# Four kinds of norm weights: broadcast loads replaced by one-row loads and products with ones

## The chip, the cores and the metric

The kernel runs on one core of one Trainium2 chip. The metric is the device time of one execution in microseconds; the time of a kernel is the median of its runs. One execution is also recorded by the hardware profiler. Its trace counts time from the start of its span, and all moments below ("at 655 us") are moments of that trace.

## The reference, cut to what matters

One layer of a streaming encoder runs over 2048 prompt rows and 128 sample rows (17 tiles of 128 rows, tile 16 being the sample rows). Half of the mixer is an HGRN2 gated recurrence, the other half is chunk-band attention. Then come an output projection, a squared-ReLU MLP and a final norm. Everything is float32. The change concerns the weights `g` of three of the norms.

```python
def rmsnorm(x, g):
    xf = x.astype(jnp.float32)
    y = xf * lax.rsqrt(jnp.mean(xf * xf, axis=-1, keepdims=True) + EPS)
    return (y * g.astype(jnp.float32)).astype(x.dtype)
...
    o_a = rmsnorm(o_a.reshape(B, T, ATT_WIDTH), att_norm_g)
    x = x + jnp.concatenate([o_h, o_a.astype(x.dtype)], axis=-1) @ w_out
    u = rmsnorm(x, norm2_g) @ w_up
    x = x + jnp.square(jax.nn.relu(u)) @ w_down
...
    y_prompt = rmsnorm(xp, final_norm_g)
    y_sample = rmsnorm(xs, final_norm_g)
```

`att_norm_g` has 512 elements, `norm2_g` and `final_norm_g` have 1024 each. Rows lie on the 128 partitions, so each weight must stand on all partitions to be multiplied in.

## The kernel before, in words

The work runs in three phases, one after the other in the program: `phase_hgrn`, `phase_att`, `phase_mlp`. Inside a phase, generators are woven together by written costs (`weave`), and the framework orders each engine's instructions from that program; every engine then runs its own list strictly in that order. Memory of a phase's pools goes to the next phase's pools, so a first write to a new tile may have to wait for the last use of an old one.

- Every large product is done in a split precision: `mm3` (L365 to L374) issues three TensorE products for each pair of a high and a low part, L370, L371 and L372. A weight block is loaded by L300 or L334 into `wraw` (2 buffers of 1024 columns), then split by ScalarE into `whi` (L321) and by VectorE into `wlo` (L322), in 8 buffers of 512 columns each.
- The recurrence, `hgrn_tile` (L545 to L667), handles one tile of 128 rows: levels of small products (L573, L580) alternate with VectorE steps on `sc`, `qp` and `ks` (L581, L594, L595), then come the output (L616, L618), the state (L621, L626), a norm (ScalarE L658, GpSimd L90 and L92) and the scaled output `ob` (L663). `c.state` is stored by L630 after the last tile.
- `phase_att` (L1052 to L1086) projects q, k and v of groups of three tiles (`att_proj_group`, from L974), runs the attention (`att_group`, from L772) and the output projection (`out_group`, L931, `out_tile`, L948), woven together. The first product of its program is the q projection of the first group. Its PSUM pool `c.ps_mm` has 3 buffers. `att_finish` (L764) multiplies each finished tile by `c.again`, the spread `att_norm_g` (L768).
- `prepare` (L1096) norms tiles of the residual with `norm2_g` (ScalarE L100, GpSimd L90 and L92, VectorE L125) and transposes them into `h_hi` and `h_lo` for the MLP (`transpose_split`, L108: TensorE L115, ScalarE L117, VectorE L118, in two halves of four transposes). For the first six tiles it runs beside the last output projection of `phase_att`, with the weight in a late tile, `g2` (L1100, L1102).
- `phase_mlp` (L1145) loads `norm2_g` once more (`c.g2`, L1159) and `final_norm_g` (`gf`, L1160), used by later `prepare` calls and by `finish` (L1164). `sample_mixer` (L1114) does the attention of the sample rows beside the first MLP group and loads `att_norm_g` again (L1119).

Before, `gain_tile` (L64) and L1102 load each weight with a DMA that reads the same row for each of the 128 partitions: 256 KB for `att_norm_g`, 512 KB for the others. There are five such loads, all on SP's queue. A second helper, `gain_rows` (L71), is used once, for the norm weights of the recurrence (`hgain`, L714): it loads one row to partition 0, then a product of a row of 128 ones with that row writes it to all partitions in PSUM (L80, `grow_ps`, 512 columns at a time), and ScalarE copies it back over the tile (L81).

Of the kernel before, what the change touches and what calls it, by code (L numbers as in the profile page):

```python
# [8 lines left out]
F32 = mybir.dt.float32  # L9
# [8 lines left out]
P = 128  # L18
D = 1024
# [33 lines left out]
def consts(c, pool):  # L53
# [5 lines left out]
    c.r1 = pool.tile([P, NTT], F32, name="r1")  # L59
    c.mhalf = pool.tile([P, 8], F32, name="mhalf")  # L60
    nc.gpsimd.memset(c.mhalf, -0.5)


def gain_tile(c, pool, name, a):  # L64
    n = a.shape[-1]
    t = pool.tile([P, n], F32, name=name)
    c.nc.sync.dma_start(out=t, in_=a.broadcast_to([P, n]))
    return t


def gain_rows(c, t, a, ps_pool, tag):  # L71
# [980 lines left out]
def phase_att(c):  # L1052
    tc, nc = c.tc, c.nc
    GMAX = max(len(x) for x in GROUPS) * P
    with ExitStack() as s:
        def pool(name, bufs, **k):
            return s.enter_context(tc.tile_pool(reuse_waits="tile", name=name, bufs=bufs, **k))
        cp = pool("a_const", 1)
        c.qsp = pool("a_qs", 4)
        c.qp_ = pool("a_q", 5)  # L1060
        c.vp = pool("a_v", NV - 3)
        c.krp = pool("a_kr", 2)
        c.ob = pool("a_ob", 2)
        c.pt = pool("a_pt", 2)
        c.sp = pool("a_s", 2)
        c.yo = pool("a_yo", 3)
        c.ps_mm = pool("a_psmm", 3, space=PSUM)
        c.ps_po = pool("a_pspo", 1, space=PSUM)
        c.ps_tx, c.ps_tx_tag = c.ps_mm, "mm"
        c.ps_s = pool("a_pss", 2, space=PSUM)  # L1070
        kw = 2 * (512 + GMAX)
        flat = c.h0p.tile([P, HN], F32R, tag="h_hi", name="K012")
        c.K = [flat[:, i * kw:(i + 1) * kw] for i in range(3)] + [cp.tile([P, kw], F32R, tag="K3", name="K3")]
        c.K = [x.rearrange("p (e n) -> p e n", e=2) for x in c.K]
        c.again = gain_tile(c, cp, "again", c.att_g)
        c.late = lambda: cp.tile([P, kw], F32, tag="K3", name="g2")[:, :D]
        gs = [Ctx() for _ in GROUPS]
        for g in gs:
            g.nk, g.nv, g.done, g.q, g.fin = 0, False, 0, [None] * 4, False

        def att():
            yield LAG
            for g, tiles in zip(gs, GROUPS):
                yield from att_group(c, g, tiles)

        run(weave(att_proj(c, gs), 19.5, att(), 13.5))  # L1086
# [9 lines left out]
def prepare(c, tiles, g, ready=None, g2=None):  # L1096
    if ready:
        while not ready():
            yield None
        g2 = g2()  # L1100
        h_tiles(c.h0p, g)
        c.nc.sync.dma_start(out=g2, in_=c.norm2_g.broadcast_to([P, D]))  # L1102
    else:
        g2 = c.g2
    for j, t in enumerate(tiles):
        x2 = c.xin.tile([P, D], F32, tag="x", name="x2")
        c.nc.sync.dma_start(out=x2, in_=c.x1[t * P:(t + 1) * P, :])
        norm_rows(c, x2, g2, x2)
        both = c.ps_s.tile([P, 2, 512], F32, tag="S", name="tx2") if ready else None
        transpose_split(c, x2, g.hi, g.lo, j * P, both=both)  # L1110
        yield 1.0


def sample_mixer(c):  # L1114

    tc, nc = c.tc, c.nc
    with ExitStack() as s:
        c.smp = s.enter_context(tc.tile_pool(reuse_waits="tile", name="s_smp", bufs=1))
        c.again = gain_tile(c, c.smp, "again", c.att_g)  # L1119
        qbd = c.smp.tile([P, 4, 8, 32], F32, name="qbd")  # L1120
        qs = c.smp.tile([P, 4, P], F32, name="qs")
        ksam = c.smp.tile([P, 4, P], F32, name="ksam")
        vsam = c.smp.tile([P, 512], F32, name="vsam")
        nc.gpsimd.memset(qbd, 0.0)
        nc.sync.dma_start(out=qs, in_=c.sq.rearrange("f p t -> p f t"))
        nc.sync.dma_start(out=ksam, in_=c.sk.rearrange("f p t -> p f t"))
        nc.sync.dma_start(out=vsam, in_=c.sv)
        for e in range(2):
            src = slice(64 * e, 64 * e + 64)
            nc.gpsimd.tensor_copy(qbd[src, :, :, 16 * e:16 * e + 16],  # L1130
                                  qs[src].rearrange("p f (b t) -> p f b t", b=8))
        yield from att_sample(c, qbd, ksam, vsam)
    with ExitStack() as s:
        op = s.enter_context(tc.tile_pool(reuse_waits="tile", name="s_oT", bufs=1))
        c.yo = s.enter_context(tc.tile_pool(name="s_yo", bufs=3))
        wp = s.enter_context(tc.tile_pool(name="s_w", bufs=4))
        o = OT(c, [14, 15, NPT])
        o.hi, o.lo = (op.tile([P, KT, 3 * P], F32R, name="sT_" + x) for x in ("hi", "lo"))
        o.pre(2)
        yield 1.0  # L1140
        for w in out_group(c, o, None, wp):
            yield 0.12 * w


def phase_mlp(c):  # L1145
# [3 lines left out]
    with ExitStack() as s:  # L1149
        def pool(name, bufs, **k):  # L1150
            return s.enter_context(tc.tile_pool(reuse_waits="tile", name=name, bufs=bufs, **k))
        cp = pool("m_const", 1)
        yp = pool("m_y", 7)
        up = pool("m_u", 1)
        wp = pool("m_u2", 2)
        c.ps_mm = pool("m_psmm", 4, space=PSUM)
        c.ps_tx, c.ps_tx_tag = pool("m_pstx", 2, space=PSUM), "tx"
        c.ps_smp = pool("m_pssmp", 2, space=PSUM)
        c.g2 = gain_tile(c, cp, "g2", c.norm2_g)  # L1159
        gf = gain_tile(c, cp, "gf", c.final_g)  # L1160

        pend = []

        def finish(t, y):  # L1164
            norm_rows(c, y, gf, y, "y")
            nc.sync.dma_start(out=rows(c, c.y_p, c.y_s, t), in_=y)

        def mlp(tiles, g):
            n = len(tiles) * P
            ys = []  # L1170
            for fc in range(DFF // FC):
                wu = next(c.ws)
                uh = up.tile([P, FC // P, GMAX], F32R, tag="uh", name="uh")
                ul = up.tile([P, FC // P, GMAX], F32R, tag="ul", name="ul")
                for f, cs, ps in proj_fm(c, wu, g, n, 1):
                    cn = cs.stop - cs.start
                    u2 = wp.tile([P, 384], F32, tag="u2", name="u2")[:, :cn]
                    nc.scalar.activation(u2, ps, AF.Relu)  # L1178
                    nc.vector.scalar_tensor_tensor(out=u2, in0=ps, scalar=0.0, in1=u2,  # L1179
                                                   op0=ALU.max, op1=ALU.mult)  # L1180
                    nc.scalar.copy(uh[:, f, cs], u2)  # L1181
                    nc.vector.tensor_tensor(out=ul[:, f, cs], in0=u2, in1=uh.bitcast(F32)[:, f, cs],  # L1182
                                            op=ALU.subtract)
                    for x in pend[:2]:
                        finish(*x)
                    del pend[:2]
                if not fc:
                    for t in tiles:
                        y = yp.tile([P, D], F32, tag="y", name="y")
                        nc.sync.dma_start(out=y, in_=c.x1[t * P:(t + 1) * P, :])  # L1190
                        ys.append(y)
                wd = [next(c.ws), next(c.ws)]
                full = slice(0, 512)
                for j, y in enumerate(ys):
                    ts = slice(j * P, (j + 1) * P)
                    for dc, w in enumerate(wd):
                        ps = c.ps_mm.tile([P, 512], F32, tag="mm", name="mm")
                        list(mm3(c, ps, [(uh[:, k, ts], ul[:, k, ts], w.hi(k, full), w.lo(k, full))
                                         for k in range(FC // P)]))
                        ysl = y[:, dc * 512:(dc + 1) * 512]  # L1200
                        nc.vector.tensor_tensor(out=ysl, in0=ps, in1=ysl, op=ALU.add)  # L1201
                    if fc == DFF // FC - 1:
                        if g.last and pend:
                            finish(*pend.pop())
                        pend.append((tiles[j], y))
                yield 1.0
            if g.last:
                finish(*pend.pop())

        h1 = Ctx()  # L1210
        c.h0.last = h1.last = False

        def side():
            yield from sample_mixer(c)
            h_tiles(pool("m_h", 1), h1)
            yield from prepare(c, GROUPS_M[1], h1)

        run(weave(mlp(GROUPS_M[0], c.h0), 17.0, side(), 26.0))
        run(weave(mlp(GROUPS_M[1], h1), 17.0, prepare(c, GROUPS_M[2], c.h0), 5.0))
        c.h0.last = True  # L1220
        run(mlp(GROUPS_M[2], c.h0))
# [105 lines left out]
```

## Time and profile before

| | us |
|---|---|
| median of 3 runs | 2972.8 (2971.18 to 2977.19) |
| the profiled execution's own time | 2972.54 |
| its span in the trace | 2970.8 |
| TensorE busy (PE) | 2891.7, 97% of the span |
| VectorE (DVE) | 1752.2, 59% |
| ScalarE (ACT) | 1111.0, 37% |
| GpSimd (POOL) | 288.1, 10% |

PE is the matmul side of TensorE, PEld its weight loads, SPq the DMA instructions issued by SyncE. "Idle before" an instruction is time in which its engine stood, with what ended it. Matmuls overlap in the pipeline, so the step from one start to the next is the price of one, not its length.

### The profile page before, as it was taken

What the parts mean: (1) busy time and instruction counts of PE and PEld (TensorE: products, weight loads), DVE (VectorE), ACT (ScalarE), POOL (GpSimd) and SP (SyncE); (2) the same over time, 40 slices, a digit from 0 to 9 for tenths busy, and PEclk for the clock granted to TensorE, in tenths of its full rate; (3) what the DMA queues carried; (4) which work ended last, traced back from release to release, by engine and by line L of the source; (5) the groups of instructions that cost most, each with busy time, mean ns of one, the idle gap of its engine ahead of it and who ended that gap; (6) DMA issues with size and microseconds to landing.
All of it is one profiled execution on the core that took longest, in us unless ns stands there. A gap on an engine that the chain in (4) does not pass through costs nothing.

```text
span 2970.8 us, 45500 instructions
## 1 busy us (share of the span) xinstructions
PE 2891.7 (97%) x18151; PEld 2626.6 (88%) x18151; DVE 1752.2 (59%) x3110; ACT 1111.0 (37%) x2256; POOL 288.1 (10%) x474
## 2 busy tenths in 40 slices
PE   8999999989999999998999999999999999999997
PEld 7888889889889899898888999999999999899997
DVE  5775775765556565656555555565555555555554
ACT  5433443435545455554223333332222223323222
POOL 3311321221010101011000000010000000000000
PEclk9999999999999999999999999999999999999999
DMA  7433323434333434447322332242212123222221
GB/s 268 163 126 113 113 97 102 137 107 140 100 125 107 128 106 140 141 156 268 114 85 87 117 98 79 72 148 65 78 57 71 57 71 128 82 75 73 84 72 64
DMA packets 119262, 328.06 MB, mean 110 GB/s; under 512 B 12613, under 2 KB 36937, under 8 KB 119050
## 3 DMA queue, kind: packets, MB, share of 16 engines
q1 hardware_dynamic: 110714, 299.20, 31.0%
q0 software_dynamic: 6320, 18.62, 1.6%
q10 hardware_dynamic: 2016, 7.34, 0.7%
q8 instruction: 142, 2.33, 0.3%
q14 instruction: 70, 0.57, 0.1%
HBM read 292.61 MB, written 32.51 MB: 109 GB/s over the span
## 4 chain that ended last, share of the span: by engine, by line
PE 73%; DVE 1%; ACT 1%; DMA 1%; issue 1%; POOL 0%; POOLq 0%; ACTq 0%; DVEq 0%
PE mm L370 22%; PE mm L372 21%; PE mm L371 21%; PE ps_oT L826 3%; PE S L819 2%; PE S L797 2%; PE tx L115 1%; ACT s L810 1%; PE ps_os L888 0%; DMA x<-x 0%; ACT junk L100 0%; DVE s L808 0%; PE tr L835 0%; ACT whi L321 0%; DVE wlo L322 0%
## 5 line engine op out<-in xcount | busy, mean ns | idle before, releaser
L321 ACT CAST whi<-wraw 128x512 fp32r<-128x512 f32 x816 | 498.0, 620 | 747.0 <-PE mm L372 537.2
L322 DVE TENSOR_TENSOR wlo<-wraw,whi 128x512 fp32r<-128x512 f32 x816 | 563.9, 708 | 238.2 <-ACT whi L321 234.3
L1201 DVE TENSOR_TENSOR y<-mm,y 128x512 f32<-128x512 f32 x544 | 373.7, 689 | 221.1 <-PE mm L372 219.4
L370 PE MATMUL mm<-h_hi,whi 128*128 128x384 f32 (+1 forms) x1536 | 503.2, 328 | 0.0
L372 PE MATMUL mm<-h_hi,wlo 128*128 128x384 f32 (+1 forms) x1536 | 501.5, 326 | 0.0
L371 PE MATMUL mm<-h_lo,whi 128*128 128x384 f32 (+1 forms) x1536 | 500.7, 326 | 0.0
L372 PE MATMUL mm<-whi,ul 128*128 128x512 f32 x1088 | 424.1, 390 | 0.0
L371 PE MATMUL mm<-wlo,uh 128*128 128x512 f32 x1088 | 424.0, 390 | 0.0
L370 PE MATMUL mm<-whi,uh 128*128 128x512 f32 x1088 | 423.5, 389 | 0.0
L370 PEld LDWEIGHTS mm<-h_hi,whi 128*128 128x128 f32 x1536 | 288.4, 188 | 4.7 <-issue 3.5
L371 PEld LDWEIGHTS mm<-h_lo,whi 128*128 128x128 f32 x1536 | 288.4, 188 | 1.2
L372 PEld LDWEIGHTS mm<-h_hi,wlo 128*128 128x128 f32 x1536 | 288.4, 188 | 0.0
L1179 DVE SCALAR_TENSOR_TENSOR u<-mm,u 128x384 f32<-128x384 f32 (+1 forms) x192 | 102.4, 534 | 278.4 <-ACT u L1178 278.3
L370 PE MATMUL mm<-hT_hi,whi 128*128 128x384 f32 (+1 forms) x768 | 259.7, 338 | 5.6 <-ACT qs L1003 4.1
L372 PE MATMUL mm<-hT_hi,wlo 128*128 128x384 f32 (+1 forms) x768 | 254.0, 331 | 0.2
L371 PE MATMUL mm<-hT_lo,whi 128*128 128x384 f32 (+1 forms) x768 | 253.4, 330 | 0.0
L372 PEld LDWEIGHTS mm<-whi,ul 128*128 128x128 f32 x1088 | 204.2, 188 | 43.1 <-DVE ul L1182 0.5
L370 PEld LDWEIGHTS mm<-whi,uh 128*128 128x128 f32 x1088 | 204.2, 188 | 41.7 <-ACT uh L1181 0.5
L371 PEld LDWEIGHTS mm<-wlo,uh 128*128 128x128 f32 x1088 | 204.2, 188 | 41.2
L1178 ACT ACTIVATE u<-mm 128x384 f32<-128x384 f32 (+1 forms) x192 | 90.4, 471 | 344.9 <-PE mm L372 344.9
L370 PE MATMUL mm<-whi,hT_hi 128*128 128x256 f32 x720 | 213.4, 296 | 0.5 <-ACT hT_hi L117 0.2
L90 POOL TENSOR_SCALAR r<-ss 128x1 f32<-128x1 f32 (+1 forms) x85 | 24.0, 283 | 1900.7 <-ACT junk L100 1675.7
(206 smaller groups left out, 4641.6 us busy)
## 6 DMA issues: line engine op xcount, KB each, us to landing
wraw<-in_w_in SPq DMA_DIRECT2D x168, 512.0 KB, 4.1
wraw<-in_w_up SPq DMA_DIRECT2D x96, 512.0 KB, 3.8
wraw<-in_w_down SPq DMA_DIRECT2D x96, 512.0 KB, 3.7
wraw<-in_w_out SPq DMA_DIRECT2D x48, 512.0 KB, 3.9
xT<-in_x_T SPq DMA_DIRECT2D x34, 512.0 KB, 4.2
og<-og SPq DMA_DIRECT2D x17, 512.0 KB, 3.5
x<-yo POOLq DMA_DIRECT2D x68, 128.0 KB, 3.3
x<-x SPq DMA_DIRECT2D x17, 512.0 KB, 4.7
```

The lines of the kernel that those rows point to most:

```text
L115: nc.tensor.transpose(ps[:, k, :], src[:, (k0 + k) * P:(k0 + k + 1) * P], c.ident)
L321: nc.scalar.copy(h, rw)
L322: nc.vector.tensor_tensor(out=l, in0=rw, in1=h.bitcast(F32), op=ALU.subtract)
L370: nc.tensor.matmul(ps, lh, rh, start=(i == 0), stop=False)
L371: nc.tensor.matmul(ps, lh, rl, start=False, stop=False)
L372: nc.tensor.matmul(ps, ll, rh, start=False, stop=(i == n - 1))
L797: nc.tensor.matmul(S[:, bk, :n], a[es, qc], c.K[ft][es, b, kc], start=(a is q and not b), stop=(a is ql))
L819: nc.tensor.transpose(ps[:, x, :], s[:, x * P:(x + 1) * P], c.ident)
L826: nc.tensor.matmul(poT[64 * e:64 * e + 64, j, :], g.vt[i - nk + 1 + x][:, 64 * h:64 * h + 64], pts[e][:, x, :], start=(x == 0), stop=(x == ...
L1178: nc.scalar.activation(u2, ps, AF.Relu)
L1179: nc.vector.scalar_tensor_tensor(out=u2, in0=ps, scalar=0.0, in1=u2, op0=ALU.max, op1=ALU.mult)
L1201: nc.vector.tensor_tensor(out=ysl, in0=ps, in1=ysl, op=ALU.add)
```

## The change

The five broadcast loads become five one-row loads, each spread by `gain_rows`, which is called and run at once at its place. `gain_tile` goes. Line numbers from `gain_rows` on are 7 lower in the changed file up to `phase_att`: L80 is L73 there, L370 to L372 are L363 to L365, L573 is L566, L580 is L573.

```diff
-def gain_tile(c, pool, name, a):
-    n = a.shape[-1]
-    t = pool.tile([P, n], F32, name=name)
-    c.nc.sync.dma_start(out=t, in_=a.broadcast_to([P, n]))
-    return t
...
 def gain_rows(c, t, a, ps_pool, tag):
     nc = c.nc
     n = a.shape[-1]
     nc.sync.dma_start(out=t[0:1, :], in_=a)
     def spread():
         for o in range(0, n, 512):
             ps = ps_pool.tile([P, 512], F32, tag=tag, name="grow_ps")
             nc.tensor.matmul(ps, c.ones[0:1, :], t[0:1, o:o + 512], start=True, stop=True)
             nc.scalar.copy(t[:, o:o + 512], ps)
     return spread
...
@@ phase_att
-        c.again = gain_tile(c, cp, "again", c.att_g)
+        c.again = cp.tile([P, 512], F32, name="again")
+        gain_rows(c, c.again, c.att_g, c.ps_mm, "mm")()
@@ prepare
-        c.nc.sync.dma_start(out=g2, in_=c.norm2_g.broadcast_to([P, D]))
+        gain_rows(c, g2, c.norm2_g, c.ps_mm, "mm")()
@@ sample_mixer
-        c.again = gain_tile(c, c.smp, "again", c.att_g)
+        c.again = c.smp.tile([P, 512], F32, name="again")
+        gain_rows(c, c.again, c.att_g, c.ps_smp, "sp")()
@@ phase_mlp
-        c.g2 = gain_tile(c, cp, "g2", c.norm2_g)
-        gf = gain_tile(c, cp, "gf", c.final_g)
+        c.g2, gf = (cp.tile([P, D], F32, name=x) for x in ("g2", "gf"))
+        for t, a in ((c.g2, c.norm2_g), (gf, c.final_g)):
+            gain_rows(c, t, a, c.ps_tx, c.ps_tx_tag)()
```

**Place one, TensorE at the end of the recurrence.** Before, the last levels of the recurrence (L580, L573, on `ps_sc`) stand among products of the next phase's q projection (`mm`, 128x384):

```order
L372 MATMUL mm<-hT_hi,wlo 128x384
L580 MATMUL ps_sc<-qp,ks 128x64 x4
L370 MATMUL mm<-hT_hi,whi 128x384
L371 MATMUL mm<-hT_lo,whi 128x384
L372 MATMUL mm<-hT_hi,wlo 128x384
L370 MATMUL mm<-hT_hi,whi 128x384
L371 MATMUL mm<-hT_lo,whi 128x384
L372 MATMUL mm<-hT_hi,wlo 128x384
L573 MATMUL ps_sc<-qp,ks 32x32 x8
L573 MATMUL ps_sc<-qp,ks 64x64 x4
L616 MATMUL ps_o<-v,sc 128x128
```

Now four levels of L580 (here L573, sixteen products) and the rest of the recurrence follow one another with nothing between them:

```order
L614 MATMUL ps_st<-v,kt 128x128 x4
L573 MATMUL ps_sc<-qp,ks 128x64 x16
L566 MATMUL ps_sc<-qp,ks 32x32 x8
L566 MATMUL ps_sc<-qp,ks 64x64 x4
L609 MATMUL ps_o<-v,sc 128x128
```

And behind the last product of the recurrence (`ps_st`) the spread of `again` comes first, then the q projection:

```order
L609 MATMUL ps_o<-v,sc 128x128
L611 MATMUL ps_o<-state,qp 128x128
L614 MATMUL ps_st<-v,kt 128x128 x4
L73 MATMUL grow_ps<-again,ones 128x512
L363 MATMUL mm<-hT_hi,whi 128x384
L364 MATMUL mm<-hT_lo,whi 128x384
L365 MATMUL mm<-hT_hi,wlo 128x384
```

All 72 products of 128x384 that stood inside the end of the recurrence have moved behind the spread; the 120 that followed it are unchanged.

**Place two, SP's queue at the same point.** Before, four weight loads go ahead of the store of `state`, three loads of `yo` and the load of `again`:

```order
L300 DMA wraw<-in_w_in 128x1024 x4
L630 DMA out<-state 128x4x128
L951 DMA yo<-in_x_prompt 128x256 x3
L67 DMA again<-in_att_norm_g 128x512
L300 DMA wraw<-in_w_in 128x1024 x2
```

Now two of the four go behind it:

```order
L293 DMA wraw<-in_w_in 128x1024 x2
L623 DMA out<-state 128x4x128
L944 DMA yo<-in_x_prompt 128x256 x3
L68 DMA again<-in_att_norm_g 1x512
L293 DMA wraw<-in_w_in 128x1024 x4
```

The load of `again` still stands behind the store of `state`, and it is now one row.

**Place three, TensorE at the start of the MLP.** Before, the last transposes of `prepare` (`tx`) are followed by the up projection (`mm` from `h_hi` and `h_lo`) without a break:

```order
L115 MATMUL tx_14537<-ident,x_14528 128x128 x4
L372 MATMUL mm<-h_hi,wlo 128x384
L370 MATMUL mm<-h_hi,whi 128x384
L371 MATMUL mm<-h_lo,whi 128x384
L372 MATMUL mm<-h_hi,wlo 128x384
L370 MATMUL mm<-h_hi,whi 128x384
```

Now the spreads of `c.g2` and `gf` stand nine products behind those transposes:

```order
L364 MATMUL mm<-h_lo,whi 128x384
L73 MATMUL grow_ps<-g_14594,ones 128x512 x2
L73 MATMUL grow_ps<-gf,ones 128x512 x2
L365 MATMUL mm<-h_hi,wlo 128x384
L363 MATMUL mm<-h_hi,whi 128x384
```

Four spread products have come in between. The spread in `prepare` (two products) stands after the first 12 products of 128x256 behind the transposes of `og`, ahead of the transposes of the first normed tile, and the one in `sample_mixer` (one product) ahead of the first L863.

## Rows read from the trace of the kernel before

**Rows 1.** Page, part 1: busy time and share of the span, instructions.
```profile
PE 2891.7 (97%) x18151; PEld 2626.6 (88%) x18151; DVE 1752.2 (59%) x3110; ACT 1111.0 (37%) x2256; POOL 288.1 (10%) x474
```
**Rows 2.** Waits of PE, 613 to 656.5 us: total us, times, longest.
```profile
PE mm L370 <- ACT qs L1003: 4.1, 1, 4.1
PE ps_sc L573 <- DVE ks L595: 1.1, 2, 0.9
PE ps_sc L580 <- DVE ks L595: 0.8, 2, 0.4
PE ps_o L616 <- ACT sc L575: 0.5, 1, 0.5
PE ps_sc L573 <- ACT sc L575: 0.3, 1, 0.3
```
**Rows 3.** Groups of PE by shape, 613 to 652 us: busy us, mean ns.
```profile
L370 PE MATMUL mm<-hT_hi,whi 128*128 128x384 f32 x24 | 8.5, 355 | 0.0
```
**Rows 4.** Timeline of PE: start, length, idle before.
```profile
634.00 0.34 PE L371 MATMUL mm<-hT_lo,whi 128*128 128x384 f32 x1
...
636.95 0.34 PE L370 MATMUL mm<-hT_hi,whi 128*128 128x384 f32 x1
...
655.99 0.44 PE L370 MATMUL mm<-hT_hi,whi 128*128 128x384 f32 x1 [4.11 <-ACT qs L1003]
```
**Rows 5.** Timeline of DVE in the last levels of the recurrence.
```profile
637.41 1.28 DVE L322 TENSOR_TENSOR wlo<-wraw,whi 128x512 fp32r<-128x512 f32 x2
...
641.38 0.44 DVE L581 COPY_PREDICATED sc<-lmask,ps_sc 128x256 f32<-128x256 uint8 x1 [0.34 <-PE ps_sc L580]
...
644.02 0.44 DVE L581 COPY_PREDICATED sc<-lmask,ps_sc 128x256 f32<-128x256 uint8 x1 [1.54 <-PE ps_sc L580]
```
**Rows 6.** Timeline of SP's queue.
```profile
655.04 0.43 SPq L67 DMA_DIRECT2D again<-in_att_norm_g  x1
```
**Rows 7.** DMA issues, 650 to 668 us: KB each, median us to landing.
```profile
yo<-in_x_prompt SPq DMA_DIRECT2D x3, 128.0 KB, 2.5
...
again<-in_att_norm_g SPq DMA_DIRECT2D x1, 256.0 KB, 4.6
...
out<-kraw SPq DMA_DIRECT2D x1, 64.0 KB, 1.5
```
**Rows 8.** Timeline of PE at the one spread that exists before.
```profile
22.30 1.12 PE L80 MATMUL grow_ps<-hgain,ones 1*128 1x512 f32 x2 [1.26 <-ACT bias L243]
23.35 0.74 PE L470 MATMUL mm<-whi,hT_hi 128*128 128x512 f32 x2
```
**Rows 9.** Windows: length; busy of PE, PEld, DVE, ACT, POOL; PEclk; DMA; GB/s.
```profile
424.00:428.00 4.00, 2.30 (x11) 1.57 (x10) 4.00 (x1) 1.07 (x3) 3.97 (x3) 1.00 0.17 66
...
645.00:656.00 11.00, 4.98 (x54) 4.40 (x53) 4.65 (x16) 4.10 (x17) 1.69 (x3) 1.00 0.17 48
...
656.00:660.00 4.00, 4.00 (x14) 4.00 (x15) 0.92 (x2) 1.48 (x4) 1.74 (x4) 0.57 0.69 214
```
**Rows 10.** Waits of PE over the whole span.
```profile
PE tx L115 <- DVE h_lo L118: 7.8, 4, 3.5
```
**Rows 11.** Timeline of ACT beside the first normed tiles.
```profile
1339.35 1.06 ACT L100 ACTIVATE junk<-x 128x1024 bf16<-128x1024 f32 x1 [2.86 <-DMA x<-x]
...
1345.01 1.06 ACT L100 ACTIVATE junk<-x 128x1024 bf16<-128x1024 f32 x1 [4.03 <-DMA x<-x]
```
**Rows 12.** Timeline of SP's queue and of PE at the MLP's start.
```profile
1371.57 0.43 SPq L67 DMA_DIRECT2D g<-in_norm_g  x1
1373.22 0.33 SPq L67 DMA_DIRECT2D gf<-in_final_norm_g  x1
...
1376.97 0.42 PE L372 MATMUL mm<-h_hi,wlo 128*128 128x384 f32 x1
```
**Rows 13.** DMA issues, 1366 to 1396 us.
```profile
g<-in_norm_g SPq DMA_DIRECT2D x1, 512.0 KB, 6.5
gf<-in_final_norm_g SPq DMA_DIRECT2D x1, 512.0 KB, 6.2
```
**Rows 14.** Waits of PE, 1376 us to the end.
```profile
PE mm L370 <- ACT sT_hi L117: 2.3, 3, 1.8
```

## The prediction

> **What bounds the kernel now.** I read the busy times first: TensorE is busy for 97% of the span [rows 1], so time is lost in two ways only, by work added to TensorE and by stretches in which it stands. The list of its waits shows where it stands. At the border of the recurrence and the attention these are five rows, 6.8 us together [rows 2], and the largest, 4.1 us, comes just before the q projection goes on at 655.99 [rows 4]. By the groups of that stretch, TensorE runs 24 products L370 of 128x384 inside the end of the recurrence [rows 3]; L371 and L372 have a row of the same shape and count there, so it is 72 products. That is three PSUM buffers of 24: the q projection fills all three of its buffers while the recurrence ends, and then stands until they are emptied. Behind 1376 us three rows of waits remain, 2.3 us for the largest and 4.1 in all [rows 14]: from there to the end TensorE never waits for a load, and what is added to it there is added to the time. The sum below is made against the profiled execution, 2972.54 us, which stands 0.3 below the median of the runs.
>
> **The price of a spread.** The one spread that exists starts at 22.30 and the product behind it at 23.35 [rows 8]: 1.05 us of TensorE for 512 columns. Eight are added, 8.4 us: one for the first `again`, two in `prepare`, four at the MLP's start, one for the sample rows.
>
> **Place one, the end of the recurrence.** The load of `again` has to wait for memory of the recurrence, its spread waits for the load, and TensorE takes its list in order, so the whole q projection is queued behind the spread. The 72 products lose their cover. From 634.00 to 636.95 seventeen steps of them take 2.95 us, 0.1735 us each [rows 4]; 72 of them are 12.5 us, which now come after the border instead of inside the waits of the recurrence. The spread adds 1.05.
>
> What does the border itself do? The chain of the recurrence gets faster without its company. Two conversions of weights took 1.28 us of VectorE among its steps, and twice VectorE waited for a level's product that stood behind ten of the 72, 0.34 and 1.54 us [rows 5]. Between nothing and their sum, 3.2, I take half, 1.6, since the conversions partly lie in the chain's own waits. The load of `again` was issued at 655.04 [rows 6], so it would go at 653.4. How long one row takes there no row shows. A 64 KB transfer landed in 1.5 us, a 128 KB one in 2.5, the broadcast of 256 KB in 4.6 [rows 7]; the three 128 KB loads stand just ahead of the row in the queue, so I take 2.5, with 1.5 and 4.6 as ends. The Trainium skill, page "DMA: Bandwidth & Descriptors", section "Anatomy of one DMA", gives a fixed 2.0 us plus bytes at 436 GB/s; by that the row takes 2.0 and the sum would be 0.5 lower, but by it the broadcast would have taken 2.6, and the row of the trace says 4.6.
>
> With 2.5 the spread starts at 655.9, within 0.1 us of where the q projection goes on today. So the wait at the border stays about as long as it is, only its reason changes from full buffers to a late row. After that wait TensorE ran at a mean of 0.57 of its clock for four us [rows 9], mostly the 1.2 GHz level; the same wait brings the same loss, and I put the difference at nothing. Place one: 12.5 + 1.05 = 13.5 us. Low end: the chain 3.2 earlier and the row in 1.5, 2.6 us less, 11. High end: the chain no earlier and the row in 4.6, 3.6 us more, 17.
>
> Two weight loads are now behind the row on SP. They feed the third weight block; two blocks are split already, 96 products or 16.7 us at 0.1735, and the longest landing among my rows is 6.5 us [rows 13]. They cost nothing, unless that landing grows beyond ten us; then the k projection is late next.
>
> **Place two, the weight in `prepare`.** The spread stands on TensorE behind 12 products and its load is issued in the middle of the attention's last group, long before, so the row is there. But the first scaling now waits for the two ScalarE copies, and these stand behind the sum of squares of the second tile, which waits for its load until 1339.35; the first half's split then stands behind the sum of squares of the third tile, which waits until 1345.01 [rows 11]. Both wait for loads that do not move. I put the second half of the first tile's transposes at 1347.3 instead of after today's longest wait, 3.5 us [rows 10]. In the meantime TensorE does the two spreads and 15 products that today come after that wait, at a low clock. By the end of the first tile it is about 0.5 us behind. I take 0.5; the low end is -2, some of the four waits of 7.8 us filled [rows 10], the high end +4, the delay of 3.9 us handed on to all later tiles.
>
> **Place three, the MLP's start.** Four spreads, 4.2 us. Their rows are issued at 1371.57 and 1373.22 [rows 12]. Even if they took as long as the 512 KB broadcasts, 6.5 and 6.2 us [rows 13], they would be there at 1378.1 and 1379.4; nine products of 0.1735 from 1376.97 [rows 12] end at 1378.5, and `gf` is wanted two spreads later, at 1380.6. So no wait, 4.2 us, all of it on the path [rows 14]. Low end 3.5, for spreads that follow each other without a gap; high end 6, for a row that lands 2 us late. The 512 KB loads that go were not waited for by TensorE there, so their absence gives nothing.
>
> **Place four, the sample rows.** One spread, 1.05 us, its row issued long before; between 0 and 2.
>
> **The sum.** 13.5 + 0.5 + 4.2 + 1.05 = 19.3 us, so 2991.8; I say **2992**. All low ends give 11 - 2 + 3.5 + 0 = 12.5 us or 2985, all high ends 17 + 4 + 6 + 2 = 29 us or 3001.5. A measurement here tells a change from none from about 0.2%, 5.9 us. The DMA traffic saved, some 2 MB, is worth nothing, because no wait of TensorE in the places concerned ends on a gain load.
>
> **Rival one: the end of the recurrence falls to the low clock.** Without the 72 products TensorE is thinly used over the last levels. At half rate the recurrence's products between 645 and 656 us, 4.98 us busy [rows 9], would take twice as long: 5 us more before the state is ready, so 2997, and up to 2999 if the levels ahead fall too. It decides if the granted clock drops before the last `ps_st`. Against it: at 424 to 428 TensorE was busy for 2.30 of 4 us and the clock stayed at 1.00, while the fall at 656 [rows 9] followed 4.1 us of standing [rows 2]. For it is the rule of the Trainium skill, page "TensorE: Matmul & The Clock Gate", section "Part 1: The HAM clock gate", that the slow state is the default and activity lifts it. The trace agrees for the full stop before 656; for thin work it speaks against. I give this rival 0.11.
>
> **Rival two, not slower: the 72 products were no filler but a burden.** If they delayed the chain of the recurrence by their whole length, the chain ends 12.5 us sooner without them, and the wait for full buffers goes as well. The most that place one can return is then all waits there, 6.8 us [rows 2], against its spread: -5.8. With 0.5 + 4.2 + 1.05 that is 0 us, 2972.5. It decides at a chain that shortens by 12.5 us. Against it: VectorE's waits for products there come to 0.34 and 1.54 us [rows 5], far from 12.5, and of TensorE's own waits inside the recurrence 1.9 of 2.7 us are for VectorE [rows 2], which does not hurry because TensorE is free. I give it 0.05, and 0.02 to anything faster still, for which the four waits in `prepare` would have to vanish too.
>
> **Rival three: the order is not what TensorE does.** If the products ran ahead of the waiting spread, their cover would stay, and only the spreads would cost: 1.05 + 0.5 + 4.2 + 1.05 = 6.8 us, so 2979. It decides if a product of the q projection starts before the spread. Against it: at 655.99 the q projection waited 4.11 us [rows 4] while nothing behind it in TensorE's list went ahead. I give it 0.02.
>
> **How the numbers follow.** The forecast has 0.80, rival one 0.11, rival two 0.05, rival three 0.02, faster still 0.02. The forecast and rivals one and three are slower by over 0.2%: 0.93. Rival two is the same: 0.05. The range goes from the sum of low ends, less 2 us for the spread of the runs, 2983, to the sum of high ends, which takes in rival one, plus 1.5 us, 3003.
>
> **What would show it.** Right: about 72 products of 128x384 more behind 655 us than now, none inside the end of the recurrence; a wait of PE for the load of `again` in place of the 4.1 us one, 4 to 7 us long; the last L621 of the recurrence 0 to 3 us earlier; four spreads in a row near the MLP's start with a step of 1.05 us and no wait; the waits of L115 together within 4 us of 7.8. Wrong: the recurrence ending 5 us or more earlier or later, a wait in front of the MLP's four spreads, or a total of L115's waits beyond 12.

## The result, and the profile after

The changed kernel takes 3009.9 us in the median of six runs (3001.97 to 3012.96), the kernel before 2976.87 beside it: a ratio of 1.0114, 95% interval 1.0102 to 1.0126, a loss of 30 to 38 us. I had forecast 2992 and a range up to 3003. The sign was right; the size was not, and the result lies outside the range. The profiled execution of the changed kernel took 3001.97 us (span 3000.2), the shortest of the six, 29.4 more span than before. It is this difference that I take apart; some 4 us of the loss by the ratio are not in it.

The page's part 1 of the changed kernel answers to [rows 1]. TensorE is 18.1 us busier with 16 more products (eight spreads, two records each); VectorE has nothing new to do.

```profile
PE 2909.8 (97%) x18167; PEld 2638.6 (88%) x18167; DVE 1753.0 (58%) x3110; ACT 1116.8 (37%) x2264; POOL 286.8 (10%) x474
```

**Place one.** The waits of PE of the changed kernel, 611 to 668 us (total, times, longest), answer to [rows 2]. The wait for full buffers has gone and a wait for the row stands in its place, as forecast. What was not forecast: the waits for VectorE's `ks` have grown from 1.9 us to 12.0.

```profile
PE ps_sc L573 <- DVE ks L588: 7.6, 4, 3.7
PE grow_ps L73 <- DMA again<-in_att_norm_g: 5.4, 1, 5.4
PE ps_sc L566 <- DVE ks L588: 4.4, 3, 2.2
```

The windows of the same stretch show why the recurrence ends late. The columns are those of [rows 9]: length, busy time of PE, PEld, DVE, ACT and POOL, granted clock, DMA share, GB/s. First the kernel before:

```profile
613.00:618.00 5.00, 4.57 (x43) 3.69 (x42) 4.99 (x9) 1.59 (x5) 1.96 (x1) 1.00 0.34 107
...
637.00:646.00 9.00, 8.14 (x60) 7.48 (x58) 6.18 (x15) 0.95 (x3) 0.17 (x1) 1.00 0.42 146
```

Then the changed kernel, whose recurrence reached the same point 1.65 us earlier:

```profile
612.00:617.00 5.00, 2.88 (x36) 2.42 (x35) 5.00 (x12) 1.36 (x4) 0.58 (x1) 1.00 0.34 107
617.00:621.00 4.00, 3.98 (x21) 3.99 (x22) 1.84 (x6) 0.47 (x1) 0.00 (x0) 0.57 0.40 134
...
637.00:646.00 9.00, 3.88 (x16) 3.56 (x16) 4.47 (x13) 0.00 (x0) 0.85 (x2) 0.55 0.07 29
646.00:656.00 10.00, 6.79 (x44) 6.24 (x45) 2.66 (x8) 1.28 (x4) 0.00 (x0) 0.50 0.01 2
```

With its filling of 72 products TensorE kept the 2.4 GHz level through the whole end of the recurrence. Without it, after 2.88 busy us of 5, it fell to 1.2 GHz at 617 us, came back, fell again at 627, came back at 635, and from 638 to 658, the start of the last `ps_st`, it stayed down. The timeline of PE (start, length, [idle before]) shows what that does to a level, and to what comes behind:

```profile
611.39 1.00 PE L573 MATMUL ps_sc<-qp,ks 128*128 128x64 f32 x8
...
639.76 1.94 PE L573 MATMUL ps_sc<-qp,ks 128*128 128x64 f32 x8 [3.67 <-DVE ks L588]
642.98 1.94 PE L573 MATMUL ps_sc<-qp,ks 128*128 128x64 f32 x8 [1.27 <-DVE ks L588]
...
657.91 1.26 PE L614 MATMUL ps_st<-v,kt 128*128 128x128 f32 x8
664.60 2.07 PE L73 MATMUL grow_ps<-again,ones 1*128 1x512 f32 x2 [5.43 <-DMA again<-in_att_norm_g]
666.60 0.69 PE L363 MATMUL mm<-hT_hi,whi 128*128 128x384 f32 x1
...
681.67 0.33 PE L363 MATMUL mm<-hT_hi,whi 128*128 128x384 f32 x1
```

The corresponding rows of the timeline before:

```profile
613.04 1.00 PE L580 MATMUL ps_sc<-qp,ks 128*128 128x64 f32 x8
...
637.64 1.08 PE L580 MATMUL ps_sc<-qp,ks 128*128 128x64 f32 x8 [0.35 <-DVE ks L595]
...
640.35 1.00 PE L580 MATMUL ps_sc<-qp,ks 128*128 128x64 f32 x8
...
642.98 1.00 PE L580 MATMUL ps_sc<-qp,ks 128*128 128x64 f32 x8
...
650.82 1.06 PE L621 MATMUL ps_st<-v,kt 128*128 128x128 f32 x8
...
659.91 0.34 PE L371 MATMUL mm<-hT_lo,whi 128*128 128x384 f32 x1
```

Eight products of a level took 1.94 us instead of 1.00, and a level went from 2.6 to 2.7 us (640.35 to 642.98, 637.64 to 640.35) to 3.2 (639.76 to 642.98). The recurrence is a chain in which TensorE and VectorE alternate, so every slow product in it lengthens it, although TensorE stands for much of the time. I count from the first level that each of the two timelines shows, here called the border. Behind the falls at 617 and 627 the chain was 4.0 us late already when the level ahead of these started: 23.70 us behind the border (635.09), before 19.71 (632.75). 681.67 is the 73rd product of the q projection, the one that started at 655.99 before [rows 4].

**Places two and three.** Timelines of PE, first the kernel before: the transposes of `og`, the first up-projection product on normed tiles, the first product with `uh`.

```profile
1330.96 0.71 PE L115 MATMUL tx<-ident,og 128*128 128x128 f32 x5
...
1373.50 0.42 PE L370 MATMUL mm<-h_hi,whi 128*128 128x384 f32 x1
...
1392.32 0.39 PE L370 MATMUL mm<-whi,uh 128*128 128x512 f32 x1
```

And the changed kernel, with the product that follows the last transposes (1376.97 before, [rows 12]) and the four spreads:

```profile
1353.31 0.82 PE L108 MATMUL tx<-ident,og 128*128 128x128 f32 x6
...
1396.07 0.42 PE L363 MATMUL mm<-h_hi,whi 128*128 128x384 f32 x1
...
1398.92 0.42 PE L365 MATMUL mm<-h_hi,wlo 128*128 128x384 f32 x1
...
1400.67 1.98 PE L73 MATMUL grow_ps<-g,ones 1*128 1x512 f32 x4
...
1404.37 0.44 PE L365 MATMUL mm<-h_hi,wlo 128*128 128x384 f32 x1
...
1419.78 0.39 PE L363 MATMUL mm<-whi,uh 128*128 128x512 f32 x1
```

Place two: 42.54 us before (1330.96 to 1373.50), 42.76 now: +0.2. Place three, from 1376.97 to 1392.32 before 15.35 us, from 1398.92 to 1419.78 now 20.86: +5.5, of which the four spreads are 3.7 (1400.67 to 1404.37). The rest is in the window behind them: TensorE busy without a gap, and yet at a mean clock of 0.72.

```profile
1399.00:1404.00 5.00, 5.00 (x19) 2.66 (x17) 0.74 (x2) 2.14 (x4) 0.04 (x1) 1.00 0.97 352
1404.00:1410.00 6.00, 6.00 (x25) 5.63 (x24) 1.11 (x2) 1.80 (x4) 0.00 (x0) 0.72 1.03 404
```

Place four: the spread of the sample rows starts at 1436.24, the next product at 1437.29: +1.05.

So two things wanted a test. One: that the end of the recurrence loses by the clock, through lost filling. Two: that products with a single row let the clock fall although TensorE is busy all the time. The rivals: that the loss comes from elsewhere (the wait for the row, the eight spreads as such), and that the fall behind the four spreads belongs to that place and not to the rows.

### The profile page after: what moved, and what is told of

Same layout as the page of the kernel before. It is cut to its first block, busy times and chain, and to the rows that moved or that the text cites. A ratio compares the mean times of both kernels' runs of the same rounds, so it can differ in the third digit from the quotient of the medians.

```text
span 3000.2 us, 45554 instructions
## 1 busy us (share of the span) xinstructions
PE 2909.8 (97%) x18167; PEld 2638.6 (88%) x18167; DVE 1753.0 (58%) x3110; ACT 1116.8 (37%) x2264; POOL 286.8 (10%) x474
## 4 chain that ended last, share of the span: by engine, by line
PE 87%; DVE 5%; DMA 3%; ACT 2%; issue 1%; POOL 1%; SPq 0%; ACTq 0%; POOLq 0%; DVEq 0%
PE mm L363 23%; PE mm L365 23%; PE mm L364 23%; PE ps_oT L819 3%; PE ps_sc L573 2%; PE S L812 2%; PE S L790 2%; PE mm L465 2%; PE mm L463 2%; PE mm L464 1%; DMA wraw<-in_w_in 1%; DVE wlo L315 1%; PE tx L108 1%; PE ps_sc L566 1%; ACT whi L314 1%
## 5 line engine op out<-in xcount | busy, mean ns | idle before, releaser
L363 PE MATMUL mm<-h_hi,whi 128*128 128x384 f32 (+1 forms) x1536 | 504.2, 328 | 0.0
L365 PE MATMUL mm<-h_hi,wlo 128*128 128x384 f32 (+1 forms) x1536 | 502.5, 327 | 0.0
L365 PE MATMUL mm<-whi,ul 128*128 128x512 f32 x1088 | 424.1, 390 | 0.0
L363 PE MATMUL mm<-whi,uh 128*128 128x512 f32 x1088 | 423.4, 389 | 0.0
L363 PEld LDWEIGHTS mm<-h_hi,whi 128*128 128x128 f32 x1536 | 289.2, 188 | 4.3 <-issue 2.6
L365 PEld LDWEIGHTS mm<-h_hi,wlo 128*128 128x128 f32 x1536 | 289.1, 188 | 0.8 <-issue 0.8
L363 PE MATMUL mm<-hT_hi,whi 128*128 128x384 f32 (+1 forms) x768 | 259.5, 338 | 2.3 <-ACT whi L314 2.2
L365 PE MATMUL mm<-hT_hi,wlo 128*128 128x384 f32 (+1 forms) x768 | 254.0, 331 | 0.3
L365 PEld LDWEIGHTS mm<-whi,ul 128*128 128x128 f32 x1088 | 204.2, 188 | 43.0 <-DVE ul L1178 0.5
L363 PEld LDWEIGHTS mm<-whi,uh 128*128 128x128 f32 x1088 | 204.3, 188 | 41.6 <-DVE u L1175 0.2
L363 PE MATMUL mm<-whi,hT_hi 128*128 128x256 f32 x720 | 212.6, 295 | 1.6 <-DVE yo L948 0.7
L365 PE MATMUL mm<-whi,hT_lo 128*128 128x256 f32 x720 | 206.5, 287 | 1.0 <-DVE hT_lo L111 1.0
```

Source lines behind the costliest of these rows:

```text
L363: nc.tensor.matmul(ps, lh, rh, start=(i == 0), stop=False)
L365: nc.tensor.matmul(ps, ll, rh, start=False, stop=(i == n - 1))
```

## The experiments

All ratios are against the kernel before, run beside each; a loss in us is the ratio's excess by its median.

**Place one alone, and all the rest.** Two kernels that split the change. The first changes `phase_att` only:

```diff
-        c.again = gain_tile(c, cp, "again", c.att_g)
+        c.again = cp.tile([P, 512], F32, name="again")
+        gain_rows(c, c.again, c.att_g, c.ps_mm, "mm")()
```

> Only the first load of att_norm_g (in phase_att) becomes a row and a spread; the four other weights stay broadcast loads. My theory now: this place carries nearly all of the loss, 22 to 28 us over before: 12.5 for the 72 products behind the spread, about 10 because the end of the recurrence runs partly at the 1.2 GHz level without them, 1 to 2 for a longer wait, 2 for the spread. The rival, that the loss over my forecast comes from the other places (MLP start, prepare), expects 13 to 15 us here. In the trace I expect the last product of the recurrence (L621) 7 to 10 us later than before, and PE waiting about 5 us for the row of again.

The second is the changed kernel with that place as before:

```diff
-        c.again = cp.tile([P, 512], F32, name="again")
-        gain_rows(c, c.again, c.att_g, c.ps_mm, "mm")()
+        c.again = gain_tile(c, cp, "again", c.att_g)
```

> The change without its first place: phase_att keeps its broadcast load of att_norm_g, the other four weights are spread. My theory: 6 to 9 us over before: 5.5 at the MLP's start (3.7 for four spreads and 1.8 for a low clock right behind them), 1 for the sample rows, about 0 in prepare. The rival, that the other places carry the excess, expects 15 to 20 us.

Measured: place one alone 2996.88 us, ratio 1.0074 (1.0061 to 1.0087), a loss of 22 us. All but it 2979.58, 1.0023 (1.0014 to 1.0033), 7 us. The two add to 29, the difference of the spans; against the 34 of the ratio that is 5 short, which their intervals cover together. Three quarters of these 29 are place one's, and its trace repeats the falls, as these windows of the first kernel show (a level starts there at 641.75, 644.97 and 648.18, again 3.2 us apart). The traced execution took 3002.91 us, the longest of its five, so I read from it only the end of the recurrence:

```profile
637.00:646.00 9.00, 3.87 (x22) 3.60 (x21) 4.55 (x14) 0.78 (x5) 1.82 (x3) 0.75 0.08 29
646.00:656.00 10.00, 5.71 (x39) 4.96 (x39) 3.70 (x10) 0.88 (x3) 0.00 (x0) 0.50 0.01 2
```

**The same work in the old order.** The whole change, but the spread in `phase_att` is kept and called in `att_finish`, right before the first use of `c.again`. The row is loaded at the same place of the program, and only TensorE's order goes back.

```diff
+    if c.spread:
+        c.spread()
+        c.spread = None
...
-        gain_rows(c, c.again, c.att_g, c.ps_mm, "mm")()
+        c.spread = gain_rows(c, c.again, c.att_g, c.ps_mm, "mm")
```

> The whole change, but in phase_att the spread of att_norm_g is issued just before its first use (the first finished attention tile) instead of at the start of the phase; the row is loaded at the same place. My theory: the 72 products go back inside the end of the recurrence, so this costs what the change without its first place costs plus one spread, 7 to 10 us over before. If instead the row load or the spread itself were what costs, wherever it stands, it stays near the change, 30 us and more over before.

Measured: 2982.3 us, ratio 1.0029 (1.0017 to 1.0041), a loss of 9 us instead of 34. The waits of PE in its trace are those of [rows 2] again, and the clock stays at the upper level until the border (it falls at 654, behind the recurrence):

```profile
PE mm L363 <- ACT qs L999: 4.1, 1, 4.1
```

```profile
637.00:646.00 9.00, 7.54 (x65) 6.98 (x63) 5.02 (x13) 1.13 (x3) 0.00 (x0) 1.00 0.32 117
646.00:656.00 10.00, 5.44 (x38) 5.18 (x37) 4.01 (x14) 4.68 (x17) 3.43 (x6) 0.94 0.33 102
```

So it is the order of the spread, not the spread, that costs at place one: the late one starts at 760.01 and the next product at 761.06, with the clock at 1.00 behind it.

**Filling put back, cover not.** The first kernel again, place one alone, with 84 products of 128x384 whose result nothing reads, six in each level of the last two tiles of the recurrence. The 72 of the q projection stay behind the spread. If the clock is what the missing filling costs, the recurrence must get its length back, while the 72 products still come late.

```diff
+        if t in (NPT - 2, NPT - 1):
+            h = c.hT[0]
+            pf = c.ps_tx.tile([P, 512], F32, tag=c.ps_tx_tag, name="fill")
+            for _ in range(NFILL):
+                nc.tensor.matmul(pf[:, :384], h[:, 0, 0:P], h[:, 1, 0:384], start=True, stop=True)
```

> As the kernel with only the first weight changed, plus 84 products of 128x384 that nobody reads, issued with the levels of the last two tiles of the recurrence; by the order 72 of them stand where the q projection's 72 stood before, the other 12 just ahead. If the granted clock is what lengthens the end of the recurrence (my theory), it ends 9 to 11 us sooner than with only the first weight changed, at a clock of 1.00, and the kernel is 8 to 13 us faster than that one, although it does 84 products more: 13 to 16 us over before. If late weight loads or anything else on SP's queue lengthen it (rival), the time stays within 3 us of the kernel with only the first weight changed, or rises by the 2 us of the 12 extra products.

Measured: 2992.42 us, ratio 1.0053 (1.0041 to 1.0065), a loss of 16. More work made it faster, by 4.5 us between the medians: its slowest execution (2994.34) is shorter than the fastest of the first kernel (2995.73). From the border to the end of the last `ps_st` its trace has 41.6 us (614.02 to 655.63), that of the first kernel 46.5 (613.84 to 660.37), the kernel before 38.8. So 4.9 of the 7.7 us by which place one alone lengthens the chain come back with the filling, and the mechanism is shown for them. But I had expected 9 to 11 of the chain and 8 to 13 of the whole. The timeline and the windows of this trace say what the filling did and did not do:

```profile
640.08 1.10 PE L581 MATMUL ps_sc<-qp,ks 128*128 128x64 f32 x8
...
642.65 1.00 PE L581 MATMUL ps_sc<-qp,ks 128*128 128x64 f32 x8
...
654.57 1.06 PE L627 MATMUL ps_st<-v,kt 128*128 128x128 f32 x8
660.97 2.07 PE L81 MATMUL grow_ps<-again,ones 1*128 1x512 f32 x2 [5.34 <-DMA again<-in_att_norm_g]
```

```profile
637.00:646.00 9.00, 8.77 (x54) 7.22 (x53) 4.53 (x13) 0.00 (x0) 1.25 (x2) 1.00 0.08 29
646.00:656.00 10.00, 7.37 (x57) 6.55 (x56) 2.95 (x9) 2.55 (x10) 0.00 (x0) 0.83 0.01 2
```

The levels are back at 1.00 us of products and 2.6 us a step. Behind the last filled level the clock fell all the same, and the last rows of the recurrence, the spread (2 us) and the first q products ran at 1.2 GHz as before. The filling gives back the levels, not the border: of the 2.8 us that the chain is still longer than before, 1.1 lie ahead of its last level (645.09), where the 84 products also stand in TensorE's list, and 1.6 behind it, where the clock fell.

**One row against 128 rows, busy in both.** The kernel before, with products of ones and `gf` whose result nothing reads, in the middle of the MLP's last group, ahead of a block of the up projection: twelve with one row, later twelve with all 128 rows, later four with one row.

```diff
+                if tiles is GROUPS_M[2] and fc in (3, 9, 13):
+                    k = 1 if fc != 9 else P
+                    for _ in range(12 if fc != 13 else 4):
+                        pb = c.ps_tx.tile([P, 512], F32, tag=c.ps_tx_tag, name="burst%d" % fc)
+                        nc.tensor.matmul(pb, c.ones[0:k, :], gf[0:k, 0:512], start=True, stop=True)
```

> The kernel before plus three bursts of products that nobody reads, between up-projection products of the last MLP group: 12 spreads' worth of one-row products (a row of ones by a row of gf, 512 columns) at the fourth block, 12 of the same size over all 128 rows (ones by gf) at the tenth, and 4 one-row ones at the fourteenth. My theory of the low clock behind the four spreads at the MLP's start: a one-row product leaves the array so idle that the clock falls although TensorE is busy. Then the granted clock falls to 0.5 in or right behind the first burst (10.5 us at full rate, 13 to 17 so), stays at 1.00 through the second, and may fall after the third. Rival: the fall at the MLP's start came from the waits ahead of it (0.8 us for a transpose) and both long bursts stay at 1.00.

Measured in one execution (3015.12 us): the windows around the first burst, which starts at 2599.04, and the second, from 2785.7 to 2796.

```profile
2595.00:2600.00 5.00, 5.00 (x21) 3.54 (x20) 3.62 (x6) 2.49 (x4) 0.00 (x0) 1.00 0.00 0
2600.00:2610.00 10.00, 10.00 (x15) 3.94 (x14) 1.46 (x3) 0.00 (x0) 0.00 (x0) 0.59 0.33 105
2610.00:2623.00 13.00, 13.00 (x33) 8.25 (x32) 0.00 (x0) 0.00 (x0) 0.00 (x0) 0.53 0.00 1
2623.00:2626.00 3.00, 3.00 (x23) 3.00 (x22) 0.98 (x2) 0.90 (x2) 0.00 (x0) 1.00 0.00 0
...
2785.00:2796.00 11.00, 11.00 (x29) 5.14 (x28) 3.25 (x6) 1.45 (x3) 0.00 (x0) 1.00 0.30 95
```

PE is busy for the whole of every row. The timeline of the three bursts, start and length:

```profile
2599.04 18.11 PE L1177 MATMUL burst<-gf,ones 1*128 1x512 f32 x24
...
2785.74 10.46 PE L1177 MATMUL burst<-gf,ones 128*128 128x512 f32 x24
...
2906.94 5.15 PE L1177 MATMUL burst<-gf,ones 1*128 1x512 f32 x8
```

With one row the clock fell just before 2602, inside the burst, and came back at 2622, behind 19 products of 128 rows; with 128 rows it never left 1.00. The same 24 passes took 18.11 us and 10.46. In the third burst, only four products of one row, it fell as well: 0.50 from 2910 to 2914. No wait stands ahead of these bursts, so the rival that a wait makes the clock fall does not explain them. A row count of one makes nothing shorter: at the upper level a pass lasts 587 ns with one row and 592 with 128.

**Place three alone, with one row and with 128.** First the kernel before with only the two weights of the MLP's start changed:

```diff
-        c.g2 = gain_tile(c, cp, "g2", c.norm2_g)
-        gf = gain_tile(c, cp, "gf", c.final_g)
+        c.g2, gf = (cp.tile([P, D], F32, name=x) for x in ("g2", "gf"))
+        for t, a in ((c.g2, c.norm2_g), (gf, c.final_g)):
+            gain_rows(c, t, a, c.ps_tx, c.ps_tx_tag)()
```

> Only the two weights at the MLP's start (norm2_g and final_norm_g, four spreads) are changed. My theory: 4 to 6.5 us over before, 3.7 for the spreads and up to 2.5 for a stretch at the lower clock behind them. Rival, spreads hidden in the waits for the transposes there: within 2 us of before.

Measured: 2979.0 us, ratio 1.0017 (1.0007 to 1.0026), a loss of 5, with the same fall behind the spreads, which end at 1386.40:

```profile
1386.00:1391.00 5.00, 5.00 (x19) 4.60 (x18) 1.11 (x2) 1.82 (x4) 0.00 (x0) 0.66 1.02 407
```

Then the same with 128 rows: the tile is zero but for its first row, and all of `c.ones` multiplies it.

```diff
+def gain_full(c, t, a, ps_pool, tag):
...
+    nc.gpsimd.memset(t, 0.0)
+    nc.sync.dma_start(out=t[0:1, :], in_=a)
...
+        nc.tensor.matmul(ps, c.ones, t[:, o:o + 512], start=True, stop=True)
...
+            gain_full(c, t, a, c.ps_tx, c.ps_tx_tag)
```

> Only the two weights at the MLP's start are changed, as in the run of place three alone (there +5.0 us, with the clock at half rate from 1386 to 1391 us behind the four one-row spreads). Here the four spreads have 128 rows instead of one: the tile is zero below its first row, and the product is with a full matrix of ones. Theory (products of one row let the clock fall although TensorE is busy): the clock stays at 1.00 over the spreads and the ten us behind them, four spreads still take 3.5 to 4.5 us, and the loss is 3 to 4.5 us, about 1.5 less than with one row. Rival (the fall has to do with the place, the switch from the transposes to the up projection, and not with the rows): the clock falls behind the spreads as before and the loss is 5 again. That the memset of 512 KB makes the row late would show as a wait of TensorE for the load in front of the first spread.

Measured: 2975.11 us, ratio 1.0005 (0.9996 to 1.0014), a loss of 1.5 that can't be told from none; the clock holds, and TensorE has no wait for the row in front of the spreads.

```profile
1378.00:1382.00 4.00, 4.00 (x13) 1.84 (x12) 0.00 (x0) 1.75 (x3) 0.00 (x0) 1.00 1.00 400
1382.00:1387.00 5.00, 5.00 (x31) 5.00 (x30) 1.12 (x2) 1.71 (x4) 0.00 (x0) 1.00 1.01 379
```

Between the same two products as at place three above, this trace has 18.88 us (1376.06 to 1394.94), +3.5, and the one with one row 20.85 (1380.95 to 1401.80), +5.5. Most of the 2 us between them is the clock's: behind the one-row spreads eleven steps, from 1386.68 to 1390.15, took 3.47 us, where 0.1735 each would be 1.91. The spreads of 128 rows stand four products later in TensorE's list than those of one row, and each kernel has one trace, so this pair alone would not decide; the bursts, which differ in the rows and have no wait near, do.

The rival that the place does it is not gone for that. In the trace of the late spread above, TensorE waited 2.15 us for the last transposes, the clock fell at 1382, ahead of the four spreads, and stayed down through them. The kernel of the next experiment has no spread here, and after a like wait its clock was down all the same (0.50 from 1378 to 1380):

```profile
1380.49 0.66 PE L108 MATMUL tx<-ident,x 128*128 128x128 f32 x4 [2.15 <-DVE h_lo L111]
...
1383.25 3.78 PE L73 MATMUL grow_ps<-g,ones 1*128 1x512 f32 x4
```

```profile
1378.11 1.12 PE L115 MATMUL tx<-ident,x 128*128 128x128 f32 x4 [2.04 <-DVE h_lo L118]
```

So the clock can fall there by the wait or by the rows, and it is dearest when the four spreads meet a clock that is down: place three took 25.63 us in the trace of the late spread (1380.90 to 1406.53), +10.3 instead of +5.5.

**The places added up.** The change without place three and with the late spread:

```diff
+        c.spread = gain_rows(c, c.again, c.att_g, c.ps_mm, "mm")
...
+        c.g2 = gain_tile(c, cp, "g2", c.norm2_g)
+        gf = gain_tile(c, cp, "gf", c.final_g)
```

> The change without place three (both weights of the MLP's start loaded by broadcast, as before), and with the spread of the attention's weight asked for in att_finish, ahead of its first use. If the places add up, what remains is 0.5 us in prepare, 1.05 us in the sample rows, and the late spread of 1.05 us: 2.5 us over before, 0 to 4, ratio 1.000 to 1.0015, and no fall of the clock in the end of the recurrence. A rival in which the late spread costs more (a fall of the clock behind a product of one row in the attention, 1.5 to 2 us as in the MLP): 4 to 5 us. If the 72 products' cover were lost in some other way than by the order, it would be 15 us or more.

Measured: 2976.19 us, ratio 1.0005 (0.9996 to 1.0014), 1.5 us over before, within the 0 to 4 expected. The places add up, as far as these intervals can tell. None of these versions beats the kernel before; the traffic saved has bought nothing in any of them.

## Why the prediction was wrong

**The step that failed is "The chain of the recurrence gets faster without its company".** It put the chain at 1.6 us shorter; it became 8.9 us longer, because without the 72 products its own products ran at 1.2 GHz for much of the way (the filled kernel shows this for 4.9 of the 7.7 us of place one alone). A second step failed with it, "I put the difference at nothing", for the clock behind the wait: the spread and the first q products ran at half rate, 3.5 us over their terms, less the 1.7 us that a fall had cost the q products there before. The prediction's own sign of being wrong came: the recurrence ended over 7 us later (659.2 against 651.9). Place one by its own steps, in the traces, both counted from the first level at the border (613.04 before, 611.39 now):

| term of place one | forecast | measured |
|---|---|---|
| chain of the recurrence, to the end of `ps_st` | -1.6 | 47.8 against 38.8: +8.9 |
| wait behind it | +1.5 | 5.4 against 4.1: +1.3 |
| the spread | 1.05 | 664.60 to 666.60: 2.0 |
| 72 products | 12.5 | 666.60 to 681.67: 15.1 |
| low clock behind the border before, now gone from the products that follow | 0 | -1.7 |
| sum | 13.5 | 25.6 |

The -1.7 is worked out from the timeline before, in which 13 steps behind 655.99 took 3.92 us at the low clock, where 0.1735 each would be 2.26; I had let that loss recur, but it falls on the 72 products now and is in their 15.1. Of the 12 us that I missed, 10.5 are the chain (8.9 longer in place of 1.6 shorter) and the rest the spread and the products at half rate. Where its products ran at the upper level the chain did get a little shorter, as forecast: 3.49 us instead of 3.61 from the border to its second level (614.88, before 616.65), and 4.67 instead of 4.89 from 635.09 to 639.76 (632.75 to 637.64). The 1.65 us by which the recurrence reached the border earlier are not the change's, and 1.6 came back in the attention, so that place two began 22.35 us late: the trace of the kernel before has two falls that the other lacks, a clock of 0.50 from 25 to 28 us and from 1251 to 1253. The changed kernel's has one of its own, behind all four places, from 1676 to 1678.

**Rival one** was this mechanism, with its place and its condition, and it was right: the clock dropped before the last `ps_st`. I gave it 0.11 and a price of 5 to 7 us. Its price was too small because I doubled only the products between 645 and 656; the levels behind 617 and 627 were hit too, 4.0 us of the 8.9, and so were the spread and the products behind the wait. Its chance was too small because of the one row I set against it, 424 to 428 at 1.00 with 2.30 us of 4 busy [rows 9]. That row shows that a thin stretch can be survived, not that it is; the end of the recurrence is a string of such stretches, 2.88 us of 5 and 3.88 of 9 among them, and the clock fell behind the first. And the row was one execution's luck. The same stretch, which no edit touches, has the same wait in the trace of place one alone, and there the clock is down behind it (0.57 from 426 to 430; in two more traces, of the filled kernel and of place three alone, 0.50). The eight products that took 0.65 us behind that wait in the kernel before took 1.09:

```profile
427.00 1.09 PE L573 MATMUL ps_sc<-qp,ks 128*64 128x64 f32 x8 [2.44 <-DVE ks L595]
```

Of the 72 products I had asked what they cost and who waits for them, and not what else they did. The page "TensorE: Matmul & The Clock Gate" of the Trainium skill, section "Part 1: The HAM clock gate", says that the slow state is the default and activity lifts it. I had written that the trace speaks against it for thin work; these runs speak for it there.

**Place three** was mis-sized by 1.3 us: forecast 4.2, measured 5.5. The four spreads were cheaper, 3.7 us, and there was no wait, as forecast; the price of a fall behind them was not in the sum, and the 10.3 of the late spread's trace show that it can be more than twice as much.

**What held.** Place two, 0.2 against 0.5, with L108's waits at 6.5 us against 7.8 [rows 10]; but that the two numbers are so close is luck. The place took 42.1 to 44.8 us in six traces without the two spreads (42.54 in the one I compare with) and 42.8 to 45.1 in four with them. Place four, 1.05. The row's landing: issued at 662.35 and used at 664.60, 2.25 us against 2.5. The 2.0 that I set beside it from the Trainium skill's page "DMA: Bandwidth & Descriptors", section "Anatomy of one DMA", lies near it too, but that section is on the path of GpSimd and this load is on SP's queue, so the agreement says little. Place one's list in order held, so rival three fell: no q product ran ahead of the spread. Rival two fell: without the products the chain got longer. That the 72 products lose their cover held as well: with the old order the loss was 9 us in all, with the new one 34.

By these traces 25.6 + 0.2 + 5.5 + 1.05 make 32.4, which lies within the 30 to 38 us of the ratio, and less the 1.65 ahead of the border and the 1.6 that came back, 29.1, against 29.4 in the spans. What stays open is the runs' own spread: the six lie 11 us apart, those of before 7, and the profiled one is the shortest. Falls of the clock that come in some executions and not in others would explain it, and the traces of the same work do differ so, at 426 us and by 5 us at place three; but no trace of a 3010 us run is at hand.

## What to carry to other kernels

Before work is moved out of a chain that alternates between TensorE and another engine, read the granted clock over that chain: its filling may hold the clock, and then moving it slows the chain itself (8.9 us here, beside the 12.5 of lost cover). A spread at the place where a phase begins puts the phase's first products behind its load; asked for at its first use, it costs its own length. And a product of one row costs as much of TensorE as one with 128, and four spreads of one row in a line can let the clock fall (behind the two in `prepare` and the one of the sample rows it stayed at 1.00), so where TensorE never waits a broadcast load that nobody waits for is the cheaper one. A clock row of one trace is one execution's: a fall that it does not show may come in the next.

## What was not expected of the hardware

That TensorE's busy time does not tell whether its clock holds. With PE busy without a gap, it fell to 1.2 GHz in a burst of 24 one-row passes and came back only behind it, while 24 passes of 128 rows left it at 2.4 GHz throughout; it fell in or behind four one-row spreads in the three traces in which it was up ahead of them, and with four of 128 rows, in one trace, it did not. And that adding 84 products whose result nobody reads can make a kernel 4.5 us faster.
